# Six weight units split in the opening, whole fp32 products for g, k, r, v of the recurrent mixer, and 512 columns in the last attention's value product

## Chip, core and metric

The kernel runs on one core of one Trainium2 chip. The metric is the device time of one execution in microseconds (us). All data is fp32; 256 tokens, 1024 features.

## The reference, cut to what matters

```
for i in range(2):                                   # first block
    sh1, sc1, gt1, sh2, sc2, gt2 = split(silu(c) @ ada_w[i] + ada_b[i], 6)
    h = rmsnorm(x, norm_g[i, 0]) * (1 + sc1) + sh1
    if i == 0:
        b, c_, hv = split(h @ conv_w_in, 3)
        y = (b * causal_conv3(c_ * hv)) @ conv_w_out
    else:                                            # recurrent mixer
        xr, xw, xk, xv, xa, xg = h + (shift(h) - h) * mu
        r, k, v = xr @ w_r, xk @ w_k, xv @ w_v
        g = sigmoid(xg @ g1) @ g2
        w, a = ...                                   # decay and gate from xw, xa
        y = (group_norm(wkv7_scan(r, w, k, v, ...)) + bonus) * g @ w_o
    x = x + gt1 * y
    h = rmsnorm(x, norm_g[i, 1]) * (1 + sc2) + sh2
    x = x + gt2 * (square(relu(h @ mlp_w1[i])) @ mlp_w2[i])
x = rmsnorm(x, final_g)
x = x + sparse_attention(rms_norm(x)); x = x + sq_relu_mlp(rms_norm(x))
k, v, f = split(rms_norm(x, g_kv) @ w_kv)            # last attention
x = x + softmax_attention(rms_norm(x, g_attn_b) @ w_q, k, v, decay(f)) @ w_o
x = rms_norm(x + sq_relu_mlp(rms_norm(x)))
```

## The kernel before

Features lie on partitions, tokens along the free axis. A weight matrix is cut into units of 128 x 1024: eight tiles of 128 x 128, one for each 128 features that are summed over (kt). Units come from HBM in pairs of 1 MB (`_dma`, L326) into the pool `raw` with two buffers. The code asks for a pair ahead of its use (`DMA_AHEAD`, 2), and all these loads stand in one queue on SP.

Nearly every product is made in three parts. `_split` (L334) rounds a unit to fp32r on ACT (L354, the high half) and subtracts it from the unit on DVE (L356, the low half), both into one buffer `HL` of the pool `hl` (four buffers). The activations are split in the same way. `mm3` (L384) then issues three fp32r products for each tile: high x high, high x low, low x high (L387 to L389). The pool buffer is given back when PE has read it, the raw buffer when DVE has split its second unit. In `rows_gen` (L412) the roles are turned: 128 tokens of the activations are the stationary operand and 256 columns of the weights stream (L423), which gives values by token.

A fp32 product that is not split is one instruction in the code and two records in the profile.

The modulation vectors (`ada`) are matrix by vector products with silu(c). Most run on DVE: one reduction of a 128 x 1024 tile gives one column (`ada_one`, L545, written as a sum in what follows; the profile shows it with a read of the accumulator behind it). Eight of them, the scale tiles of the first layer, run on PE (`ada_pe`, L558): eight tiles of 128 x 128 against a column of silu(c).

The opening, `conv_start` (L581): eight steps, one for each kt. A step sums a scale tile on PE and a shift tile on DVE, makes a column of gain on DVE (L617), normalizes x (L619), makes z on ACT (L621), its high half on ACT (L622) and its low half on DVE (L623). The first six weight units are loaded into tiles of their own (`hs`) and multiplied whole, as fp32, with the whole z (`zf`, L630), as far as the step allows. Then the ordinary loop of the conv goes on with unit 6.

The recurrent mixer, `rwkv` (L1133): the front normalizes x and makes h and its difference to the token before, xx. `mixed` (L1193) makes one kt of an input: xx * mu + h on DVE (L1194), its high half on ACT (L1195), its low half on DVE for g and on POOL for k, r and v (L1196). The units come in the order g (2), k (8), r (8), v (8), then w_o (8). Each k output starts a chain of short steps (`decay`, `front`; the scans are L1253), each r output another (`back`, which begins with L1358), each pair of v outputs starts `values`, which waits for copies and products on POOL (L1452, L1455) and issues L1459, L1467 and L1473 on PE. `inverse` inverts 32 x 32 blocks on DVE, 31 steps of two instructions (L1423, L1425), with transposes at its start (L1418) and end (L1428, L1430). When the inverse and all values are there, eight `state` chains run, four at a time (L1493 is their first product). Between the unit pairs of the mixer, pairs of `ada` tiles for the second layer are loaded into `raw` as well; DVE reduces them where the scheduler finds room.

The last attention, `fox` (L1042): its values are made by `rows_gen` in four groups of 256 columns, from two units each.

The code issues generators side by side; the order on each engine is then set by a list scheduler with priorities. Instructions of an engine run in that order.

## Time and profile before

| | |
|---|---|
| median of 3 runs | 1436.61 us (1433.08 to 1442.31) |
| profiled execution | 1441.53 us |
| its span in the profile | 1439.8 us |
| PE, DVE, ACT, POOL busy | 94%, 71%, 54%, 12% of the span |
| HBM read | 257.69 MB, 180 GB/s over the span |

The profile is of one execution. PE is TensorE, DVE is VectorE, ACT is ScalarE, POOL is GpSimd; SP issues the loads. Times within it are from the start of the span. "L356" is line 356 of the kernel before. Busy shares are means over all stages.

### The profile page before, as it was taken

The numbers are of one execution on the slowest core, as the hardware profiler recorded it, in microseconds if no ns is written. First come the engines' busy times: TensorE is split into PE (matmuls) and PEld (weight loads), VectorE is DVE, ScalarE is ACT, GpSimd is POOL, SyncE is SP. The second block draws the span as 40 slices with busy tenths as digits, with TensorE's granted clock in tenths as the row PEclk, the third lists the DMA queues.
The fourth block names the chain that finished last, engine by engine and source line by source line (L and its number), as shares of the span: only waits on it lengthen the run. The fifth ranks groups of instructions, "written<-read, shape, count | busy, mean of one in ns | idle before, by whom it ended". The sixth has DMA issues, their size and how long they took to land.

```text
span 1439.8 us, 26749 instructions
## 1 busy us (share of the span) xinstructions
PE 1357.8 (94%) x10724; PEld 1303.4 (91%) x10724; DVE 1019.3 (71%) x1959; ACT 772.5 (54%) x1480; POOL 172.8 (12%) x181
## 2 busy tenths in 40 slices
PE   7999999998879869999999998999999999999997
PEld 6899899997779868989999986899999997899997
DVE  3499998756999886678566679765556759565554
ACT  2345664843756431248367555665474557573663
POOL 0000000003783422010000073000000000000000
PEclk9899999998999988999999999999999999999999
DMA  9488888552235552156555543255555651365552
GB/s 371 159 333 286 308 309 303 192 189 104 74 118 197 192 168 74 59 176 212 176 181 197 179 142 117 97 196 185 179 196 182 214 193 64 122 217 188 179 195 97
DMA packets 46908, 263.43 MB, mean 183 GB/s; under 512 B 5472, under 2 KB 9776, under 8 KB 20800
## 3 DMA queue, kind: packets, MB, share of 16 engines
q1 hardware_dynamic: 46432, 260.97, 51.8%
q8 instruction: 84, 1.38, 0.4%
q0 software_dynamic: 208, 0.59, 0.1%
q14 instruction: 40, 0.33, 0.1%
q10 hardware_dynamic: 144, 0.16, 0.0%
HBM read 257.69 MB, written 2.11 MB: 180 GB/s over the span
## 4 chain that ended last, share of the span: by engine, by line
PE 72%; DVE 15%; DMA 4%; POOL 4%; ACT 2%; issue 2%; POOLq 0%; DVEq 0%; SPq 0%; ACTq 0%
PE mm L388 18%; PE mm L387 18%; PE mm L389 18%; DVE HL L356 4%; DMA raw<-in_w_dram 3%; DVE adu L545 2%; PE mm L630 1%; PE ax L558 1%; PE mm L423 1%; PE ax L423 1%; PE ax L847 1%; ACT HL L354 1%; PE ax L630 1%; PE ax L840 1%; POOL R L1455 1%
## 5 line engine op out<-in xcount | busy, mean ns | idle before, releaser
L356 DVE TENSOR_TENSOR HL<-raw,HL 128x1024 fp32r<-128x1024 f32 x372 | 458.1, 1238 | 229.5 <-ACT HL L354 229.0
L354 ACT ACTIVATE HL<-raw 128x1024 fp32r<-128x1024 f32 x372 | 389.4, 1056 | 295.6 <-PE mm L389 221.3
L389 PE MATMUL mm<-zh,HL 128*128 128x256 f32 (+1 forms) x1328 | 376.1, 284 | 5.9 <-DVE HL L356 5.8
L387 PE MATMUL mm<-zh,HL 128*128 128x256 f32 (+1 forms) x1328 | 376.8, 284 | 4.4 <-DVE x L701 1.6
L388 PE MATMUL mm<-zl,HL 128*128 128x256 f32 (+1 forms) x1328 | 375.1, 283 | 0.0
L388 PE MATMUL mm<-hlo,HL 128*128 128x256 f32 x1024 | 287.9, 281 | 0.1
L389 PE MATMUL mm<-hh,HL 128*128 128x256 f32 x1024 | 287.6, 281 | 0.0
L387 PE MATMUL mm<-hh,HL 128*128 128x256 f32 x1024 | 285.3, 279 | 0.0
L387 PEld LDWEIGHTS mm<-zh,HL 128*128 128x128 f32 x1328 | 251.3, 189 | 8.4 <-issue 3.8
L389 PEld LDWEIGHTS mm<-zh,HL 128*128 128x128 f32 x1328 | 251.5, 190 | 7.6 <-DVE HL L356 7.6
L388 PEld LDWEIGHTS mm<-zl,HL 128*128 128x128 f32 x1328 | 252.2, 190 | 0.0
L387 PEld LDWEIGHTS mm<-hh,HL 128*128 128x128 f32 x1024 | 193.3, 189 | 0.0
L388 PEld LDWEIGHTS mm<-hlo,HL 128*128 128x128 f32 x1024 | 192.5, 188 | 0.3 <-DVE hlo L746 0.3
L389 PEld LDWEIGHTS mm<-hh,HL 128*128 128x128 f32 x1024 | 192.4, 188 | 0.0
L515 POOL TENSOR_TENSOR r<-r,mhalf 128x2 f32<-128x2 f32 x6 | 6.3, 1046 | 682.4 <-DVE r L510 545.6
L387 PE MATMUL mm<-yh,HL 128*128 128x256 f32 x272 | 80.1, 297 | 8.2 <-ACT yh L1195 3.9
L545 DVE CUSTOM_DVE_ANT_0 adu<-adu,cact,cols 128x1024 f32<-128x1024 f32 x64 | 81.2, 1280 | 2.0 <-DMA adu<-in_ada_dram 2.0
L388 PE MATMUL mm<-yl,HL 128*128 128x256 f32 x272 | 78.9, 292 | 0.0
L389 PE MATMUL mm<-yh,HL 128*128 128x256 f32 x272 | 78.1, 288 | 0.0
L387 PEld LDWEIGHTS mm<-yh,HL 128*128 128x128 f32 x272 | 52.5, 194 | 10.4 <-ACT yh L1195 4.5
L746 DVE TENSOR_TENSOR hlo<-ma,hh 128x256 fp32r<-128x256 f32 x128 | 53.5, 421 | 5.8 <-ACT hh L743 3.1
L743 ACT ACTIVATE hh<-ma 128x256 fp32r<-128x256 f32 x128 | 52.9, 417 | 3.5
(437 smaller groups left out, 2246.5 us busy)
## 6 DMA issues: line engine op xcount, KB each, us to landing
raw<-in_w_dram SPq DMA_DIRECT2D x187, 1024.0 KB, 5.0
adu<-in_ada_dram SPq DMA_DIRECT2D x72, 512.0 KB, 8.1
raw<-in_ada_dram SPq DMA_DIRECT2D x12, 1024.0 KB, 5.0
hs<-in_w_dram SPq DMA_DIRECT2D x3, 1024.0 KB, 12.6
cb<-cd SPq DMA_DIRECT2D x1, 2048.0 KB, 9.0
rs<-raw SPq DMA_DIRECT2D x28, 64.0 KB, 2.2
x<-in_x_dram SPq DMA_DIRECT2D x4, 256.0 KB, 4.6
R<-in_wa_dram SPq DMA_DIRECT2D x2, 512.0 KB, 6.5
```

What stands on the lines that cost most here:

```text
L354: s.nc.scalar.activation(h, raw, AF.Copy)
L356: s.nc.vector.tensor_tensor(l, raw, h.bitcast(F32), op=OP.subtract)
L387: mm(ps, H[:, kt], rh, start=start, stop=False)
L388: mm(ps, H[:, kt], rl, start=False, stop=False)
L389: mm(ps, L[:, kt], rh, start=False, stop=stop)
L423: s.nc.tensor.matmul(ps[j][:, :256], a, b[:, k], start=kt == i == 0, stop=kt == 7 and i == 2)
L545: s.nc.vector.tensor_tensor_reduce(t, t, s.cact, scale=1.0, scalar=s.c("adab", i), op0=OP.mult, op1=OP.add, accum_out=s.modf[:, i:i + 1])
L558: s.nc.tensor.matmul(ps, w[:, k], s.ccol[:, k:k + 1], start=k == 0, stop=k == KT - 1)
L630: mm(tiles[i][:, :T], w[:, k], zf[:, k], start=k == 0, stop=k == KT - 1)
L743: nc.scalar.activation(s.hh[:, m], a, AF.Copy)
L746: nc.vector.tensor_tensor(s.hlo[:, m], a, s.hh[:, m].bitcast(F32), op=OP.subtract)
L840: tr(pt[:, 128 * j:128 * j + 128], lg[e][:, 128 * j:128 * j + 128], s.ident)
```

## The change

Three edits. In the opening, the six first units are now split like all others (four into the tiles `hs`, two into `HL`), and go through `mm3` with the split z; the products follow z by two steps (`PLAG`). Three of the eight scale tiles (steps 3, 5, 7) are summed on DVE and not on PE. In the recurrent mixer, the 26 units of g, k, r and v are not split: a pair is loaded straight into a buffer of the pool `hl` (named `rawh`), up to three pairs ahead, and multiplied whole, as fp32, with unsplit inputs xg, xk, xr, xv; the copies on ACT and the subtractions on DVE and POOL that split these inputs are gone. In the last attention, the value product runs in two groups of 512 columns.

```diff
-ADAPE = range(8)
+ADAPE = (0, 1, 2, 4, 6)
+PLAG = 2
...
-def row_units(w):
+def row_units(w, n=256):
-    u = w.reshape(2, 4, 128, -1, 256).transpose(3, 0, 2, 1, 4)
+    u = w.reshape(n // 128, D // n, 128, -1, n).transpose(3, 0, 2, 1, 4)
...
-        s.R[p] = s.rawx.pop(p) if p in s.rawx else s.raw.tile([128, 2, D], F32, name="raw")
         n, i = s.pairs[p]
+        if n == "w" and 2 * p in s.whole:
+            s.R[p] = s.hl.tile([128, 2, D], F32, name="rawh", tag="HL")
+        else:
+            s.R[p] = s.raw.tile([128, 2, D], F32, name="raw")
...
-        while s.dma_to <= min(p + s.DMA_AHEAD - 1, len(s.pairs) - 1):
+        while s.dma_to <= min(p + (3 if u in s.whole else s.DMA_AHEAD) - 1, len(s.pairs) - 1):
             s._dma()
         s.split_to += 1
         if s.pairs[p][0] == "ada":
             return
-        if u < s.whole:
+        if u in s.whole:
...
+        if L is None:
+            mm(ps, H[:, kt], rh, start=start, stop=stop)
+            return
...
-    def rows_gen(s, n, z, evac):
+    def rows_gen(s, n, z, evac, N=256):
         for m in range(n):
             ps = [s.mmbank() if RB[(2 * m + j) % len(RB)] else s.axbank() for j in range(2)]
-            for q in range(2):
-                H, L = (w.rearrange("p (k a) m -> p k (a m)", a=2) for w in s.unit())
-                for k in range(4):
-                    kt = 4 * q + k
+            for q in range(N // 128):
+                H, L = (w if w is None else w.rearrange("p (k a) m -> p k (a m)", a=N // 128) for w in s.unit())
+                for k in range(D // N):
+                    kt = D // N * q + k
                     for j in range(2):
-                        zh, zl = (y[:, kt, 128 * j:128 * j + 128] for y in z)
-                        for i, (a, b) in enumerate(((zh, H), (zh, L), (zl, H))):
-                            s.nc.tensor.matmul(ps[j][:, :256], a, b[:, k], start=kt == i == 0, stop=kt == 7 and i == 2)
+                        zs = [y[:, kt, 128 * j:128 * j + 128] for y in z]
+                        ab = [(zs[0], H)] if L is None else [(zs[0], H), (zs[0], L), (zs[1], H)]
+                        for i, (a, b) in enumerate(ab):
+                            s.nc.tensor.matmul(ps[j][:, :N], a, b[:, k], start=kt == i == 0,
+                                               stop=kt == 7 and i == len(ab) - 1)
...
-        hs = [s.big.tile([128, 2, 2, D], F32, name=f"hs{i}", tag=f"h{i}") for i in range(2)]
-        s.rawx = {p: hs[p // 2][:, p % 2] for p in range((GN + 1) // 2)}
-        s.whole = GN
+        hs = [s.big.tile([128, 2, 2, KT, 128], F32R, name=f"hs{i}", tag=f"h{i}") for i in range(2)]
+        s.hlx.update({u: hs[u // 2][:, u % 2] for u in range(4)})
...
-        for kt in range(KT):
-            pm = s.axbank()
-            s.ada_pe(st[kt][0], pm[:, :1])
-            s.ada_one(st[kt][1], 8 + kt)
-            loads(kt + CSP + 1)
-            g = s.gp[:, 0, kt:kt + 1]
-            V.scalar_tensor_tensor(g, pm[:, :1], a1[:, kt:kt + 1], s.c("ng", kt), op0=OP.add, op1=OP.mult)
-            t = s.t("z0")
-            V.tensor_tensor(t, s.x[:, kt], s.rstd[:, :T], op=OP.mult)
-            z = zf[:, kt]
-            A.activation(z, t, AF.Identity, bias=s.mod[:, 0, 1, kt:kt + 1], scale=g)
-            A.activation(s.zh[:, kt, :T], z, AF.Copy)
-            V.tensor_tensor(s.zl[:, kt, :T], z, s.zh[:, kt, :T].bitcast(F32), op=OP.subtract)
-            while len(units) < GN and kt >= CSW[len(units) // 2]:
-                units.append(s.unit(0)[0])
-                at.append(0)
+        for kt in range(KT + PLAG):
+            if kt < KT:
+                g = s.gp[:, 0, kt:kt + 1]
+                if kt in ADAPE:
+                    pm = s.axbank()
+                    s.ada_pe(st[kt][0], pm[:, :1])
+                    V.scalar_tensor_tensor(g, pm[:, :1], a1[:, kt:kt + 1], s.c("ng", kt), op0=OP.add, op1=OP.mult)
+                else:
+                    s.ada_dve(st[kt][0], kt)
+                    V.scalar_tensor_tensor(g, s.modf[:, kt:kt + 1], 1.0, s.c("ng", kt), op0=OP.add, op1=OP.mult)
+                s.ada_one(st[kt][1], 8 + kt)
+                loads(kt + CSP + 1)
+                t = s.t("z0")
+                V.tensor_tensor(t, s.x[:, kt], s.rstd[:, :T], op=OP.mult)
+                z = zf[:, kt]
+                A.activation(z, t, AF.Identity, bias=s.mod[:, 0, 1, kt:kt + 1], scale=g)
+                A.activation(s.zh[:, kt, :T], z, AF.Copy)
+                V.tensor_tensor(s.zl[:, kt, :T], z, s.zh[:, kt, :T].bitcast(F32), op=OP.subtract)
+                while len(units) < GN and kt >= CSW[len(units) // 2]:
+                    units.append(s.unit(0))
+                    at.append(0)
             for i, w in enumerate(units):
-                while at[i] <= kt:
+                while at[i] <= kt - PLAG:
                     k = at[i]
-                    mm(tiles[i][:, :T], w[:, k], zf[:, k], start=k == 0, stop=k == KT - 1)
+                    s.mm3(tiles[i][:, :T], w, k, s.zh[:, k, :T], s.zl[:, k, :T], k == 0, k == KT - 1)
...
-            s.drive(s.rows_gen(4, (zh, zl), ev_vv), per=PERF)
+            s.drive(s.rows_gen(2, (zh, zl), ev_vv, 512), per=PERF)
...
-            gh, gl = s.yh, s.yl
-            new = lambda n, tags, w=T: [s.big.tile([128, KT, w], F32R, name=n + q, tag=q) for q in tags]
-            xkh, xkl = new("xk", ("zh", "zl"), T + 2)
-
-            def mixed(n, kt, hi, lo_, on=None):
-                t = s.t("mx")
-                V.scalar_tensor_tensor(t, xx[:, kt], s.c("mu", 8 * n + kt), h[:, kt, 1:], op0=OP.mult, op1=OP.add)
-                A.activation(hi[:, kt, :T], t, AF.Copy)
-                (on or eng("ml")).tensor_tensor(lo_[:, kt, :T], t, hi[:, kt, :T].bitcast(F32), op=OP.subtract)
-
-            def mixes(n, hi, lo_):
+            new = lambda n, tag: s.big.tile([128, KT, T], F32, name=n, tag=tag)
+            xg, xk, xr = new("xg", "yh"), new("xk", "zh"), new("xr", "yl")
+
+            def mixed(n, kt, out):
+                V.scalar_tensor_tensor(out[:, kt], xx[:, kt], s.c("mu", 8 * n + kt), h[:, kt, 1:], op0=OP.mult, op1=OP.add)
+
+            def mixes(n, out):
                 for kt in range(KT):
-                    mixed(n, kt, hi, lo_)
+                    mixed(n, kt, out)
...
-            s.drive(s.linear_gen(2, lambda k: gh[:, k], lambda k: gl[:, k], ev_g, head=2),
-                    mixes(2, xkh, xkl), per=1)
-            xrh, xrl = new("xr", ("yh", "yl"))
-            side = s.spawn(mixes(0, xrh, xrl))
-            s.linear(8, lambda k: xkh[:, k, :T], lambda k: xkl[:, k, :T], ev_k, head=2, per=PERK)
+            none = lambda k: None
+            s.drive(s.linear_gen(2, lambda k: xg[:, k], none, ev_g, head=2), mixes(2, xk), per=1)
+            side = s.spawn(mixes(0, xr))
+            s.linear(8, lambda k: xk[:, k], none, ev_k, head=2, per=PERK)
...
-            s.linear(8, lambda k: xrh[:, k], lambda k: xrl[:, k], ev_r, head=2, per=PERR)
+            s.linear(8, lambda k: xr[:, k], none, ev_r, head=2, per=PERR)
...
-            s.drive(s.rows_gen(4, (xv[:, 0], xv[:, 1]), ev_v), per=PERV, alone=True)
+            s.drive(s.rows_gen(4, (xv,), ev_v), per=PERV, alone=True)
...
+            us = [u for u in range(s.start["rwkv"], 2 * len(s.pairs)) if s.pairs[u // 2][0] == "w"]
+            s.whole |= set(us[:26])
```

The scheduler then orders the program anew. Three places, all on DVE. First the opening, from the second step's sum on; `z`, `zf`, `zh` and `zl` are as above, `adu` is a modulation tile, `gp` the gain. Before:

```order
L545 ISA adu,mod<-adu,cact,cols 128x1024
L545 ISA mod 128x1
L623 TENSOR_TENSOR zl<-zf,zh 128x256
L545 ISA adu,mod<-adu,cact,cols 128x1024
L545 ISA mod 128x1
L617 SCALAR_TENSOR_TENSOR gp<-ax,a_136,cols 128x1 x2
L623 TENSOR_TENSOR zl<-zf,zh 128x256
L545 ISA adu,mod<-adu,cact,cols 128x1024
L545 ISA mod 128x1
L623 TENSOR_TENSOR zl<-zf,zh 128x256
L545 ISA adu,mod<-adu,cact,cols 128x1024
L545 ISA mod 128x1
```

The same place of the changed kernel (its L553 is L545 of before, L638 is L623, L627 is L617, L359 is L356, L630 is the gain column of a tile summed on DVE):

```order
L553 ISA adu,mod<-adu,cact,cols 128x1024
L553 ISA mod 128x1
L638 TENSOR_TENSOR zl<-zf,zh 128x256
L359 TENSOR_TENSOR hs_114<-raw,hs_114 128x1024
L627 SCALAR_TENSOR_TENSOR gp<-ax,a_138,cols 128x1
L359 TENSOR_TENSOR hs_114<-raw,hs_114 128x1024
L553 ISA adu,mod<-adu,cact,cols 128x1024
L553 ISA mod 128x1
L553 ISA adu,mod<-adu,cact,cols 128x1024
L553 ISA mod 128x1
L638 TENSOR_TENSOR zl<-zf,zh 128x256
L630 SCALAR_TENSOR_TENSOR gp<-mod,cols 128x1
```

The two splits of the first pair stand around a gain column, and the sum of step 3 behind the one of step 2.

Second, the start of the k part of the mixer; `gA` is the scan's output, `mx` an input of k or r, `gs` the gate g, `th` and `Sd` belong to the decay. Before:

```order
L1253 SCALAR_TENSOR_TENSOR gA<-one_3618,th 128x64 x4
L1255 TENSOR_TENSOR Sd<-gA 128x260
L1194 SCALAR_TENSOR_TENSOR mx<-hx,cols 128x256
L1259 TENSOR_TENSOR PC<-Sd,gA 128x3
L1194 SCALAR_TENSOR_TENSOR mx<-hx,cols 128x256
L356 TENSOR_TENSOR HL<-raw,HL 128x1024
L1194 SCALAR_TENSOR_TENSOR mx<-hx,cols 128x256 x4
L1317 TENSOR_SCALAR gs<-gt 128x256 x2
L1194 SCALAR_TENSOR_TENSOR mx<-hx,cols 128x256 x4
L356 TENSOR_TENSOR HL<-raw,HL 128x1024
L1253 SCALAR_TENSOR_TENSOR gA<-one_3618,th 128x64 x4
```

The same place now (L1263 is L1253 of before, L1265 is L1255, L1327 is L1317, `raw` is a modulation tile):

```order
L1263 SCALAR_TENSOR_TENSOR gA<-one_3700,th 128x64 x4
L553 ISA raw,mod<-raw,cact,cols 128x1024
L553 ISA mod 128x1
L1265 TENSOR_TENSOR Sd<-gA 128x260
L553 ISA raw,mod<-raw,cact,cols 128x1024
L553 ISA mod 128x1
L1269 TENSOR_TENSOR PC<-Sd,gA 128x3
L1327 TENSOR_SCALAR gs<-gt 128x256
L553 ISA raw,mod<-raw,cact,cols 128x1024
L553 ISA mod 128x1
L1327 TENSOR_SCALAR gs<-gt 128x256
L553 ISA raw,mod<-raw,cact,cols 128x1024
```

The mixes have moved ahead of the scan (all eight of r stand there), the splits are gone, and modulation sums stand in their place.

Third, the end of the inverse; `it` and `ya` are its steps, `hk` its result. Before:

```order
L545 ISA raw,mod<-raw,cact,cols 128x1024
L545 ISA mod 128x1
L1423 TENSOR_TENSOR it<-ya 128x60
L545 ISA raw,mod<-raw,cact,cols 128x1024
L545 ISA mod 128x1
L1425 TENSOR_TENSOR ya<-ya,it 128x2x30
L1423 TENSOR_TENSOR it<-ya 128x31
L1425 TENSOR_TENSOR ya<-ya,it 128x31
L1428 STREAM_TRANSPOSE hk<-ya 128x32x32
L1430 STREAM_TRANSPOSE hk<-ya 128x32x32
```

The same place now (L1432 is L1423 of before, L1434 is L1425, L1461 is L1452, L1437 and L1439 the transposes):

```order
L1434 TENSOR_TENSOR ya<-ya,it 128x3x29
L1432 TENSOR_TENSOR it<-ya 128x60
L1434 TENSOR_TENSOR ya<-ya,it 128x2x30
L1432 TENSOR_TENSOR it<-ya 128x31
L1461 COPY yb<-R 64x4x64
L1434 TENSOR_TENSOR ya<-ya,it 128x31
L1437 STREAM_TRANSPOSE hk<-ya 128x32x32
L1461 COPY yb<-R 64x4x64
L1439 STREAM_TRANSPOSE hk<-ya 128x32x32
```

The sums are gone from between the steps; two copies for the last values stand there.

## Rows read from the trace of the kernel before

**Rows 1.** Busy time by stage: start:end, length, each engine's busy us (instructions), clock, DMA.

```profile
14.00:64.00 50.00, 47.15 (x224) 40.63 (x224) 19.66 (x43) 12.00 (x22) 0.00 (x0) 0.86 0.60 245
64.00:150.00 86.00, 80.51 (x657) 78.43 (x656) 80.10 (x146) 42.53 (x72) 0.00 (x0) 1.00 0.88 317
150.00:336.00 186.00, 181.68 (x1517) 180.61 (x1517) 144.87 (x222) 107.15 (x172) 3.87 (x6) 1.00 0.70 247
336.00:358.00 22.00, 17.09 (x81) 14.66 (x82) 15.40 (x36) 9.79 (x23) 8.71 (x17) 0.77 0.26 103
358.00:421.00 63.00, 49.81 (x347) 43.22 (x346) 59.84 (x127) 40.25 (x99) 52.13 (x57) 0.95 0.23 79
421.00:470.00 49.00, 48.40 (x419) 48.08 (x420) 46.30 (x87) 34.89 (x93) 20.98 (x23) 1.00 0.55 201
470.00:527.00 57.00, 40.98 (x303) 40.12 (x304) 49.84 (x103) 22.96 (x61) 23.80 (x15) 0.87 0.58 191
...
925.00:1120.00 195.00, 194.74 (x1646) 194.52 (x1645) 121.26 (x169) 115.75 (x196) 0.00 (x0) 1.00 0.56 190
```

**Rows 2.** The chain that ended last, opening: start us, us, what.

```profile
48.47 5.61 PE ax L630 x26
```

**Rows 3.** Groups by line: busy us, mean ns of one, idle before.

```profile
L356 DVE TENSOR_TENSOR HL<-raw,HL 128x1024 fp32r<-128x1024 f32 x372 | 458.1, 1238 | 229.5 <-ACT HL L354 229.0
L354 ACT ACTIVATE HL<-raw 128x1024 fp32r<-128x1024 f32 x372 | 389.4, 1056 | 295.6 <-PE mm L389 221.3 <-DMA raw<-in_w_dram 65.3 <-PE ax L423 8.1
...
L545 DVE CUSTOM_DVE_ANT_0 adu<-adu,cact,cols 128x1024 f32<-128x1024 f32 x64 | 81.2, 1280 | 2.0 <-DMA adu<-in_ada_dram 2.0
```

**Rows 4.** Timeline of the opening: start us, us, engine, line, what [idle before].

```profile
13.99 6.83 PE L558 MATMUL ax<-ccol,adu 128*128 128x1 f32 x32
...
19.63 0.33 SPq L331 DMA_DIRECT2D hs<-in_w_dram  x1
...
24.39 0.43 DVE L623 TENSOR_TENSOR zl<-zf,zh 128x256 fp32r<-128x256 f32 x1 [1.12 <-ACT zh L622]
...
26.68 4.01 PE L558 MATMUL ax<-ccol,adu 128*128 128x1 f32 x32
...
28.94 0.22 DVE L617 SCALAR_TENSOR_TENSOR gp<-ax,a,cols 128x1 f32<-128x1 f32 x1 [2.92 <-PE ax L558]
...
61.07 2.36 DVE L356 TENSOR_TENSOR HL<-raw,HL 128x1024 fp32r<-128x1024 f32 x2 [0.52 <-ACT HL L354]
```

**Rows 5.** DMA issues of the page: issues, KB each, median us to landing.

```profile
raw<-in_w_dram SPq DMA_DIRECT2D x187, 1024.0 KB, 5.0
```

**Rows 6.** k part alone, by line: splits L356, mixes L1194, sums L545, subtractions L1196.

```profile
358.00:421.00 63.00, 14.05 (x10) 0.95 0.23 79
...
358.00:421.00 63.00, 7.77 (x13) 0.95 0.23 79
...
358.00:421.00 63.00, 3.52 (x4) 0.95 0.23 79
...
358.00:421.00 63.00, 0.00 (x0) 13.12 (x15) 0.95 0.23 79
```

**Rows 7.** Waits in the value part, 470 to 527: us in total, times, longest.

```profile
PE ax L1493 <- DVE hk L1430: 8.8, 1, 8.8
...
PE ax L1459 <- POOL R L1455: 7.2, 3, 2.7
```

**Rows 8.** The chain that ended last, end of the value part: start us, us, what.

```profile
506.04 0.71 POOL yb L1452
...
506.87 0.79 POOL yb L1452
...
507.72 3.32 POOL R L1455
...
526.72 3.75 PE ax L1493 x16
...
533.36 0.89 PE ax L1500 x8
```

More of the change, by code (lines that the diff above doesn't have):

```diff
@@ L38 @@
 VW = 0
-ML5 = [0, 0, 0, 0, 0, 0, 0, 0]
 ADE = [0, 0]
@@ L42 @@
 RB = [1, 0]
-ENG = {'db': 1, 'zb': 1, 'ta': 0, 'kr': 1, 'ts': 1, 's1': 0, 'yl': 0, 'sd': 0, 'kp': 1, 'rk': 0, 'zk': 0, 'ab': 1, 's0': 1, 'ml': 1}
+ENG = {'db': 1, 'zb': 1, 'ta': 0, 'kr': 1, 'ts': 1, 's1': 0, 'yl': 0, 'sd': 0, 'kp': 1, 'rk': 0, 'zk': 0, 'ab': 1, 's0': 1}
 GN = 6
-ADAPE = range(8)
+ADAPE = (0, 1, 2, 4, 6)
 CSP = 4
 CSW = [1, 3, 5]
+PLAG = 2
 HLB = 4
@@ L166, in fox_units @@
     w = I["w_kv_b_2"]
-    return (units_of(w[:, :D]) + row_units(w[:, D:2 * D]) + units_of(I["w_q_b_2"][0]) + units_of(I["w_o_b_2"][0]))
+    return (units_of(w[:, :D]) + row_units(w[:, D:2 * D], 512) + units_of(I["w_q_b_2"][0]) + units_of(I["w_o_b_2"][0]))
 def att_consts():
@@ L347, in _split @@
             pool = s.hle if u < s.early and u % 3 == 2 and HLE else s.hl
-            t = pool.tile([128, 2, KT, 128], F32R, name="HL")
+            t = pool.tile([128, 2, KT, 128], F32R, name="HL", tag="HL")
         s.H[u], s.L[u] = t[:, 0], t[:, 1]
@@ L542, in ada_load, with ada_dve, ada_one @@
         return t
-    def ada_one(s, t, i):
+    def ada_dve(s, t, i):
         s.nc.vector.tensor_tensor_reduce(t, t, s.cact, scale=1.0, scalar=s.c("adab", i), op0=OP.mult, op1=OP.add,
                                          accum_out=s.modf[:, i:i + 1])
+    def ada_one(s, t, i):
+        s.ada_dve(t, i)
         q, part = i % 8, i // 8 % 6
@@ L1096, in ev_vv @@
                 for j in range(2):
-                    A.activation(vr[:, 2 * m:2 * m + 2, j], ps[j][:, :T].rearrange("p (a n) -> p a n", a=2), AF.Copy,
+                    A.activation(vr[:, 4 * m:4 * m + 4, j], ps[j].rearrange("p (a n) -> p a n", a=4), AF.Copy,
                                  scale=s.rcol[:, j:j + 1])
-            s.drive(s.rows_gen(4, (zh, zl), ev_vv), per=PERF)
+            s.drive(s.rows_gen(2, (zh, zl), ev_vv, 512), per=PERF)
             s.new_y()
@@ L1186, in rwkv @@
             s.norm_close()
-            s.new_y()
-            gh, gl = s.yh, s.yl
-            new = lambda n, tags, w=T: [s.big.tile([128, KT, w], F32R, name=n + q, tag=q) for q in tags]
-            xkh, xkl = new("xk", ("zh", "zl"), T + 2)
-            def mixed(n, kt, hi, lo_, on=None):
-                t = s.t("mx")
-                V.scalar_tensor_tensor(t, xx[:, kt], s.c("mu", 8 * n + kt), h[:, kt, 1:], op0=OP.mult, op1=OP.add)
-                A.activation(hi[:, kt, :T], t, AF.Copy)
-                (on or eng("ml")).tensor_tensor(lo_[:, kt, :T], t, hi[:, kt, :T].bitcast(F32), op=OP.subtract)
-            def mixes(n, hi, lo_):
+            new = lambda n, tag: s.big.tile([128, KT, T], F32, name=n, tag=tag)
[3 more added lines that the diff above has]
+            def mixes(n, out):
                 for kt in range(KT):
-                    mixed(n, kt, hi, lo_)
+                    mixed(n, kt, out)
                     yield None
@@ L1218, in rwkv @@
                 mm(pl[:, :T], wam[:, kt], xx[:, kt], start=False, stop=kt == KT - 1)
-                mixed(5, kt, gh, gl, (V, G)[ML5[kt]])
+                mixed(5, kt, xg)
             A.activation(lo[0:64], pl[0:64, :T], AF.Tanh)
@@ L1344, in mix_v @@
                     s.finish_gen(fro[p])
-                xv.append(s.big.tile([128, 2, KT, T], F32R, name="xv", tag="h1"))
+                xv.append(new("xv", "h1"))
                 for kt in range(KT):
-                    mixed(3, kt, xv[0][:, 0], xv[0][:, 1])
+                    mixed(3, kt, xv[0])
                     yield WV
@@ L1635, in run @@
         s.feed = lambda kt: None
-        s.hlx, s.rawx, s.whole = {}, {}, 0
+        s.hlx, s.whole = {}, set()
+        if "rwkv" in s.start:
+            us = [u for u in range(s.start["rwkv"], 2 * len(s.pairs)) if s.pairs[u // 2][0] == "w"]
+            s.whole |= set(us[:26])
         s.early = next((s.start[n] for n in stages if n not in ("conv", "mlp0")), 2 * len(s.pairs))
```

## Prediction

> **What bounds the kernel now.** I read the page first, then the busy time by stage, then the groups, and last the timeline, the waits and the chain of the stages that the change touches. On the page PE is busy nearly throughout, but that is a mean over stages that differ [rows 1]. In the plain matmul stages, such as 925 to 1120, PE does nothing but stream: 1646 records in 194.74 us, 0.118 us for one product of 256 columns. In 14 to 64, the opening, PE is busy 47.15 of 50 us and DVE 19.66: PE sets the pace. In 64 to 150, the conv, DVE is busy 80.10 of 86: DVE sets the pace, so whatever the opening gains or loses is handed on. From 150 to 336 PE is full again and DVE has 41 us free. The recurrent mixer has four parts: its front (336 to 358, a chain of short steps), the k part (358 to 421, DVE 59.84 of 63), the r part (421 to 470, PE 48.40 of 49, DVE nearly as full) and the value part (470 to 527, DVE 49.84 of 57, PE full for a part only). After 527 eight states run, a chain of short PE and DVE steps.
>
> **Price of one product.** A whole fp32 product of 256 columns is two records. Twenty-six of them back to back took 5.61 us, 0.216 us each [rows 2], so a product costs 0.43 us against 3 x 0.118 = 0.35 for the three split ones. A unit of eight costs PE 0.63 us more whole, and spares DVE 1.24 and ACT 1.06 us of splitting [rows 3].
>
> **The opening, term 1: -5 us.** PE loses three of eight modulation sums (two tiles took 4.01 us [rows 4], so 6 us in all) and 6 x 0.63 = 4 us of products, and is no longer the bound. DVE gets three sums at 1.28 and six splits at 1.24, 11 us, and becomes it. I follow its new order with the durations of the rows. ACT can split unit 0 only behind z of step 1 (that step's subtraction starts at 24.39 [rows 4]), so its high half is there at 25.5; the third tile's sum stands behind the first product of it on PE, and at the pace of PE's first two sums (6.83 us for two) it ends at 28.9. That is where the third gain column came before, 28.94, so to there nothing is won. Then DVE splits unit 1 (to 30.4), which frees the raw buffer. Of two raw buffers, the third pair of units therefore goes out at 30.4, not at 19.63 [rows 4]; it lands some 5 us later [rows 5] and the four modulation tiles queued behind it on SP by about 40.5. DVE wants the first of them near 49, so this is hidden by 8 us. From 30.4 DVE has nine sums (11.5 us), six splits (7.4), six subtractions of 0.43 (2.6) and five columns of 0.22 (1.1), 22.6 us up to the split of unit 7. Three of the subtractions wait 1.12 us for ACT, as the one at 24.39 does; the others stand behind a second sum. Three pairs of splits wait another 0.6. That is 22.6 + 5.2, and ends at 58.2. Before, the same split ended at 61.07 + 2.36 = 63.43. I take -5. The ends are -10 (no wait at all) and 0 (PE at its slow level throughout, so that each column comes late).
>
> **The mixer's front, term 2: +2 us.** 24 mixes instead of 11 now stand ahead of the first scan: 13 x 0.6 = 7.8 us at the k part's mean [rows 6], less eight subtractions of 0.43, and one modulation sum stands ahead of the norm's factor. DVE was busy 15.40 of 22 us [rows 1], so most of these 4 to 6 us goes into its gaps. Bounds 0 and +5.5.
>
> **The k part, term 3: -2 us.** DVE loses ten splits, 14.05 us [rows 6], and eleven mixes at 0.6, 6.6 us. But where four records of modulation sums stood there (two sums, 3.52 us), the new order has fifteen. At 1.28 us each, as where POOL is quiet, the thirteen add 16.6 us; at the 1.76 of this part they add 22.9. So DVE changes by -4 to +2. POOL loses fifteen subtractions, 13.12 of its 52.13 us, which leaves DVE alone more often. I take -2. PE's work grows by some 92 whole products for 276 split ones, 92 x 0.076 = 7 us, in a part where it is busy 49.81 of 63; DVE hides it.
>
> The sums took 1.76 us each beside a busy POOL here [rows 6] and 1.28 in the mean of all in the span [rows 3]. The Trainium skill, SBUF, section "Who interferes with whom", says that a DVE instruction with two SBUF inputs is held off for the whole of a GpSimd instruction that reads SBUF and has started first. That speaks against moving sums into this part. The trace agrees in kind: 0.48 us more, about half of a mean POOL instruction (52.13 us for 57, 0.91 each). The full hold is the first rival.
>
> **The r part, term 4: +6 us.** PE is the bound, and between the first product of an r back end and the first of a value step the order has 180 split products before and 64 whole ones now: 27.5 - 21.2 = +6.3. DVE loses seven splits and three of six sums by its order, but it was not alone at the limit and can give PE little. Bounds 0 (DVE was as tight as PE) and +8.
>
> **The value part, term 5: -11.5 us.** Before, it ran from 469.1 to 526.72. PE's last wait in it is 8.8 us for the inverse on DVE [rows 7]. Fourteen modulation sums and five splits stood between the inverse's steps, and now three splits do: DVE has 14 x 1.28 + 2 x 1.24 = 20.4 us less to do, and the inverse ends near the last values. The value steps before that took 48.8 us in four rounds; in each PE waited for POOL, 7.2 us in three waits [rows 7], since two copies (0.71 and 0.79 us) and two products (3.32 us) on POOL stand between two rounds, about 5 us with their hand-overs [rows 8], and PE had only 36 products (4.2 us) to put there. Now it has twelve whole ones, 5.2 us: most of the 44 x 0.43 - 132 x 0.118 = +3.3 us goes into these waits. Rounds of 12.5, 12.5, 12 and 7 us give 44, and about 2 more until the state starts. So 46 instead of 57.6. Ends: -5.5 (the rounds stay as long and get the 3.3 us) and -15 (no waits left).
>
> **The states, term 6: -2.5 us.** After the long wait PE ran at 1.2 GHz: sixteen records took 3.75 us, against 0.89 for eight at 2.4 GHz a little later [rows 8]. With that wait gone some 24 records win 0.12 us each. Three splits and two sums on DVE go too, in a chain that waits for DVE only in part. Bounds -5 and +1.
>
> **The last attention's values, term 7: -1 us.** 192 products of 256 columns cost 192 x 0.118 = 22.7 us, and 96 of 512 columns cost between 96 x 0.216 (a record that streams as many columns) and 96 x 0.236: -1.9 to 0. The Trainium skill, TensorE: Matmul & The Clock Gate, section "Back-to-back issue gap", puts N columns at N / 2.4 + 2.5 ns, an estimate of 0.216 us; by it the term would be -1.9 and the total one us lower. No row shows a product of 512 columns.
>
> Sum: -5 + 2 - 2 + 6 - 11.5 - 2.5 - 1 = -14. The profiled execution took 1441.5 us (span 1439.8 and 1.7 around it), 4.9 above the median of the runs; it would take 1427.5, and the median 1436.6 - 14 = 1422.6.
>
> **Rivals.** (a) POOL holds each of the thirteen sums for a whole instruction: 13 x (1.28 + 0.91) = 28.5 us less 20.6 that go, and the k part grows by 8 instead of falling by 2: -4, 1432.6. For it: DVE is in order and the scans behind the sums feed ACT and PE. Against: rows 6 show 1.76. Chance 0.1. (b) PE stays the bound in the value part too: term 5 is -5.5 and the states win nothing: -5.5, 1431. For it: PE was busy 89 of the 106 us of both parts [rows 1] and now gets 9.6 us more in a shorter time. Chance 0.14. (c) More is won: the k part's chain of short steps was slowed by POOL as a whole and gives 8 us, and the opening 8: -23, 1413.6. Chance 0.2. (d) Slower: SP is one queue. Whole tiles wait there for a buffer that PE frees, the next pair of sums is loaded behind them, and the sums stand in DVE's order ahead of scans. If DVE reaches a pair before PE has freed the tile, DVE and all behind it wait out a load of 5 us; six pairs give +30, and the total is +16, 1452.6. It decides as soon as PE frees a pair of k tiles less often than DVE takes two sums, every 8.4 us (63 us for fifteen). Against: PE was busy 49.81 us of the 63 [rows 1] and gets 7 more, so it still has room. Chance 0.08.
>
> **How the numbers follow.** The forecast (-14, its own range -7 to -21, 1415.6 to 1429.6) has 0.48. The range 1409 to 1437 takes in (a), (b) and most of (c), leaves (d) out and about one case in ten at the lower end. About 1%, 14.4 us, can be told from no change: 1422.2 is that bound. Of the forecast 0.27 lies below it and 0.21 above; (c) is faster; (a) and (b) are within; (d) is slower. Faster 0.47, same 0.45, slower 0.08.
>
> **What would show it.** The first split product of the ordinary conv loop near 58 to 60 us, right behind the split that ended at 63.43 before (term 1). First scan of the mixer to first r back end 60 to 63 us long, with sums at 1.3 to 1.7 us (term 3). From there to the first value step about 54 us (term 4), and the state's first product 46 us after that with a wait under 2 us ahead of it (term 5). Wrong would be: DVE waiting for a DMA of modulation tiles in the k part, a wait for the inverse that stays, or a conv stage that no longer follows the opening.

## The result, and the profile after

The changed kernel took 1426.85 us (median of 7 runs, 1418.36 to 1428.91) against 1439.44 us for the kernel before beside it: ratio 0.991 (95% interval 0.9886 to 0.9933), 12.6 us less. A second series of it (9 runs, below) gave 1426.69 us and 0.9922 (0.9896 to 0.9947). 1422.6 was forecast. The total fell close to the forecast; its terms did not, as the stages show.

The changed kernel, busy time by stage, columns as in [rows 1]; the stretches begin and end where the same instructions do as there, the last but one is the eight `state` chains, called the states from here on:

```profile
14.00:64.00 50.00, 42.79 (x250) 41.52 (x249) 33.05 (x59) 18.75 (x30) 0.00 (x0) 1.00 0.69 259
64.00:150.00 86.00, 80.66 (x651) 79.15 (x652) 80.67 (x149) 43.26 (x72) 1.68 (x1) 0.98 0.87 315
331.20:353.20 22.00, 15.81 (x64) 12.92 (x65) 18.67 (x45) 5.71 (x13) 8.49 (x16) 0.77 0.45 177
353.20:417.70 64.50, 53.38 (x255) 42.77 (x253) 53.05 (x132) 26.96 (x75) 40.73 (x49) 0.94 0.63 228
417.70:474.40 56.70, 56.14 (x361) 52.90 (x362) 34.77 (x82) 23.48 (x74) 6.09 (x7) 0.95 0.27 93
474.40:514.70 40.30, 39.56 (x266) 36.53 (x264) 34.10 (x67) 21.53 (x61) 11.22 (x15) 1.00 0.17 57
514.70:558.60 43.90, 41.47 (x323) 38.17 (x324) 30.25 (x75) 8.13 (x22) 9.94 (x8) 1.00 0.15 46
905.00:1100.00 195.00, 194.86 (x1646) 194.64 (x1646) 121.35 (x170) 115.86 (x197) 0.00 (x0) 1.00 0.55 189
```

Four readings. In the opening DVE is busy 33.05 us instead of 19.66 and PE 42.79 instead of 47.15, at a granted clock of 1.00 instead of 0.86. In the k part neither PE (53.38 of 64.5) nor DVE (53.05, it was 59.84 of 63) is full any more, and yet it is not shorter. In the r part PE is full, 56.14 of 56.7. In the value part PE is full too, 39.56 of 40.3, where it had 40.98 of 57. The plain matmul stage of the last row is as it was.

The profiled execution is the fastest of the seven (1418.36 us, span 1416.6). The profile of the second series (1429.77 us, span 1428.0) is of the slowest of its nine, 3.1 us above their median, so the sizes of the parts are read from both. "k part" is from the first scan to the first r back end, "r part" from the first product of that back end to the first value step, "value part" from there to the state's first product, "states" to the end of the last product of that line (L1493, now L1502). The half microsecond between the k part's end on DVE and the r part's start on PE is in neither.

| us | before | after, 1st | after, 2nd | 2nd - before | forecast |
|---|---|---|---|---|---|
| start to first scan | 358.0 | 353.2 | 356.9 | -1.1 | -3 (terms 1, 2) |
| k part | 62.6 | 64.5 | 64.8 | +2.2 | -2 |
| r part | 48.0 | 56.1 | 58.4 | +10.4 | +6 |
| value part | 57.6 | 40.3 | 40.3 | -17.3 | -11.5 |
| states | 52.2 | 43.9 | 49.8 | -2.4 | -2.5 |
| behind the states | 860.9 | 858.0 | 857.3 | -3.6 | -1 |
| span | 1439.8 | 1416.6 | 1428.0 | -11.8 | -14 |

The value part in the profile after, PE's first products of each round (start us, us, engine, line, what, idle before):

```profile
474.39 1.95 PE L1468 MATMUL ax<-R,yb 128*128 128x128 f32 x16
...
486.21 1.95 PE L1468 MATMUL ax<-R,hk 128*128 128x128 f32 x16
...
498.03 1.95 PE L1468 MATMUL ax<-R,yb 128*128 128x128 f32 x16
...
508.66 0.46 PE L1468 MATMUL ax<-R,hk 128*128 128x128 f32 x2 [0.37 <-ACT hk L1453]
...
514.67 1.16 PE L1502 MATMUL ax<-hk,ed 128*128 128x128 f32 x8 [0.27 <-DVE R L1477]
```

Rounds of 11.8, 11.8, 10.6 and 6.0 us: this is PE's own work, with no wait for POOL. Where PE stood 8.8 us for the inverse [rows 7], 0.27 us are left.

### The profile page after: what moved, and what is told of

It reads as the page before. It is cut to its first block, busy times and chain, and to the rows that moved or that the text cites. A ratio compares the mean times of both kernels' runs of the same rounds, so it can differ in the third digit from the quotient of the medians.

```text
span 1416.6 us, 26025 instructions
## 1 busy us (share of the span) xinstructions
PE 1349.4 (95%) x10420; PEld 1290.1 (91%) x10420; DVE 994.1 (70%) x1937; ACT 742.4 (52%) x1424; POOL 132.9 (9%) x157
## 4 chain that ended last, share of the span: by engine, by line
PE 76%; DVE 13%; POOL 3%; DMA 3%; issue 2%; ACT 2%; POOLq 0%; DVEq 0%; SPq 0%; ACTq 0%
PE mm L394 19%; PE mm L393 19%; PE mm L395 19%; DVE HL L359 3%; PE mm L391 2%; DVE adu L553 2%; PE mm L430 2%; PE ax L430 1%; DMA raw<-in_w_dram 1%; DMA adu<-in_ada_dram 1%; PE ax L569 1%; PE ax L862 1%; POOL R L1321 1%; PE ax L1372 1%; DMA rs<-raw 1%
## 5 line engine op out<-in xcount | busy, mean ns | idle before, releaser
L359 DVE TENSOR_TENSOR HL<-raw,HL 128x1024 fp32r<-128x1024 f32 x348 | 426.8, 1233 | 226.0 <-ACT HL L357 225.7
L357 ACT ACTIVATE HL<-raw 128x1024 fp32r<-128x1024 f32 x348 | 364.3, 1056 | 281.5 <-PE mm L395 214.9
L553 DVE CUSTOM_DVE_ANT_0 adu<-adu,cact,cols 128x1024 f32<-128x1024 f32 x67 | 84.9, 1280 | 0.6 <-DMA adu<-in_ada_dram 0.6
L393 PE MATMUL mm<-yh,HL 128*128 128x256 f32 x256 | 75.5, 297 | 3.1 <-DVE x L718 2.2
L394 PE MATMUL mm<-yl,HL 128*128 128x256 f32 x256 | 74.2, 292 | 0.0
L395 PE MATMUL mm<-yh,HL 128*128 128x256 f32 x256 | 73.8, 289 | 0.0
```

The costliest lines, as they stand in the source:

```text
L357: s.nc.scalar.activation(h, raw, AF.Copy)
L359: s.nc.vector.tensor_tensor(l, raw, h.bitcast(F32), op=OP.subtract)
L393: mm(ps, H[:, kt], rh, start=start, stop=False)
L394: mm(ps, H[:, kt], rl, start=False, stop=False)
L395: mm(ps, L[:, kt], rh, start=False, stop=stop)
L553: s.nc.vector.tensor_tensor_reduce(t, t, s.cact, scale=1.0, scalar=s.c("adab", i), op0=OP.mult, op1=OP.add, accum_out=s.modf[:, i:i + 1])
```

## The experiments

Each kernel was timed in five rounds beside the kernel before; a difference to before in us is the ratio less one, times the median of before in that series. A difference between two changed kernels is that of their medians.

### The three edits one by one

open_alone is the kernel before with this and what belongs to it in the opening:

```diff
-ADAPE = range(8)
+ADAPE = (0, 1, 2, 4, 6)
+PLAG = 2
...
+        s.hlx.update({u: hs[u // 2][:, u % 2] for u in range(4)})
...
+                    s.mm3(tiles[i][:, :T], w, k, s.zh[:, k, :T], s.zl[:, k, :T], k == 0, k == KT - 1)
```

> The kernel before with the opening edit alone (six split tiles, five sums on PE, lag of two). Theory A, the parts are separate: the shift of 4 us that the two traces show from 60 us on is made here and carried to the end, so -4 us against before (-3 to -5.5). Rival B: the front of the mixer waits for something of its own, so that the shift is lost at 340 us: -1 to +1 us. The first split product of the conv loop behind a split that ends near 60.6 us in both.

1433.96 us against 1440.29: 0.9965 (0.9944 to 0.9985), -5.0 us. Theory A. Its first scan stands at 354.3 us, 3.7 early.

mixer_alone is the kernel before with the mixer's edit:

```diff
+            s.whole |= set(us[:26])
...
-            s.linear(8, lambda k: xkh[:, k, :T], lambda k: xkl[:, k, :T], ev_k, head=2, per=PERK)
+            s.linear(8, lambda k: xk[:, k], none, ev_k, head=2, per=PERK)
```

> The kernel before with whole g, k, r, v products in the mixer alone. Theory A, the parts add up: of -12.6 us in the medians 4 are the opening's and 1 to 2 the last attention's, so -7 us here (-5 to -10), made of about +2 in the k part, +5 to +8 in the r part and -17 in the value part. Rival B, the opening is worth nothing by the end: -11 to -13 us here.

1426.96 us: 0.9914 (0.9886 to 0.9943), -12.4 us: B's size, though B's reason, an opening that is worth nothing, is against open_alone. Its k, r and value part took 64.6, 56.1 and 40.3 us, as in the whole change: these are the mixer's own. Its first scan stands at 358.2 us, against 358.0 before, so the longer front of the mixer costs nothing that shows.

fox_alone is the kernel before with this:

```diff
-    return (units_of(w[:, :D]) + row_units(w[:, D:2 * D]) + ...
+    return (units_of(w[:, :D]) + row_units(w[:, D:2 * D], 512) + ...
...
-            s.drive(s.rows_gen(4, (zh, zl), ev_vv), per=PERF)
+            s.drive(s.rows_gen(2, (zh, zl), ev_vv, 512), per=PERF)
```

> The kernel before with 512 columns in the last attention's value product alone. The products themselves: 96 x 0.230 against 192 x 0.118 us is -0.5 us. Theory A: only that, -0.5 us (0 to -1). Rival B: the 2.4 us by which the two traces differ near 1240 us come from this edit too (PE's two waits at the start of the last MLP, 1.3 and 0.7 us, go): -2.4 us (-1.8 to -3).

1440.29 us: 0.9999 (0.998 to 1.0017), nearer to theory A; the interval, -2.9 to +2.4 us, does not exclude B. The two waits near 1240 us, 1.3 and 0.7 us before, are down to 0.4 in its trace, but they are 0.2 in mixer_alone and gone in sums_early, which do not have this edit.

The parts give -17.4 us, the whole -11 to -13: the intervals allow both sums. xv_no_open, below, asks again.

### What shortened the value part

Two things changed there at once: the products are whole, and the modulation sums are gone. Each was tried without the other. sums_late is the changed kernel with the pairs of sums in the buffers of the whole tiles, in stream order:

```diff
-        if n == "w" and 2 * p in s.whole:
+        if n == "ada" or 2 * p in s.whole:
```

> The changed kernel with the pairs of modulation tiles in the buffers of the whole tiles, so that they queue in the order of the stream and 17 of the sums stand between the steps of the inverse again. Theory A, the value part shrank because these sums left DVE there: 17 x 1.28 = 22 us come back to a DVE that is busy 34 of 40 us, the value part goes from 40 to about 54 us, the k part gains at most 2, and the kernel is 10 us slower than the changed one (8 to 14), within 3 us of before. Rival B, it shrank because whole products fill PE's waits for POOL and five splits are gone, whatever DVE does between: within 2 us of the changed kernel.

1437.26 us: 0.9978 (0.9958 to 0.9997), 10.4 us above the changed kernel. The value part and the states of sums_late, by stage:

```profile
471.60:525.70 54.10, 40.31 (x266) 36.57 (x264) 50.64 (x96) 22.30 (x62) 17.03 (x15) 0.94 0.58 202
525.70:579.90 54.20, 52.28 (x323) 46.45 (x324) 32.30 (x79) 7.69 (x20) 9.94 (x8) 0.78 0.09 30
```

DVE is busy 50.64 of 54.10 us again, as it was before, and PE's waits in the value part show the inverse (L1439) again, but little of POOL, which before took 7.2 us of them:

```profile
PE ax L1502 <- DVE hk L1439: 8.5, 1, 8.5
...
PE ax L1468 <- POOL R L1464: 1.5, 1, 1.5
```

Theory A, with the value part and the total where it had them (about 54 us, and 10 slower).

sums_early is the kernel before, split products and all, with the twelve pairs ahead of the units of k and r:

```diff
-ADAPOS = [0, 0, 0, 0, 0, 1, 0, 1, 1, 1, 0, 0, 7, 1, 0, 0, 0]
+ADAPOS = [0, 0, 2, 2, 2, 2, 2, 2, 0, 0, 0, 0, 0, 0, 0, 0, 0]
```

> The kernel before, with split products as before, but the twelve pairs of modulation tiles placed ahead of the units of k and r, so that no sum stands between the steps of the inverse. Theory A, what shortened the value part is that the sums left it: value part 57.6 to about 46 us (42 to 49), the wait for the inverse gone and the slow-clock stretch in the states with it (states 44 to 46 instead of 52), while k and r part grow by 8 to 18 together, since DVE is as good as full there with the splits in it; in all -4 us against before (-10 to +3). Rival B, whole products are what shortens it: value part 54 us or more.

1442.63 us against 1439.08: 1.0035 (1.001 to 1.0061), +5.0 us. Theory A in the mechanism, but only there: the value part is shorter still than its 42 to 49 us, the k and r part grow by more than its 8 to 18, the states do not fall to 44 to 46, and the total lies outside its range. sums_early by stage, k part to states:

```profile
359.30:433.00 73.70, 57.12 (x317) 48.35 (x316) 68.03 (x139) 39.16 (x97) 62.37 (x62) 0.72 0.35 122
433.00:490.20 57.20, 51.39 (x441) 50.45 (x440) 53.49 (x100) 36.67 (x92) 18.92 (x18) 1.00 0.61 212
490.20:528.90 38.70, 37.01 (x310) 35.94 (x308) 37.41 (x79) 25.38 (x66) 11.24 (x15) 1.00 0.38 119
528.90:582.50 53.60, 50.84 (x323) 44.92 (x324) 31.13 (x76) 7.68 (x20) 9.94 (x8) 0.81 0.11 34
```

In its value part PE waits 1.1 us for DVE and 0.4 us for ACT, and for POOL not at all.

The four kernels side by side, from one profile each; the two with whole products have the new opening as well, which ends ahead of these parts:

| us | k part | r part | value part | sum |
|---|---|---|---|---|
| split, sums late (before) | 62.6 | 48.0 | 57.6 | 168.2 |
| split, sums early | 73.7 | 56.6 | 38.7 | 169.0 |
| whole, sums late | 62.8 | 58.3 | 54.1 | 175.2 |
| whole, sums early (the change) | 64.5 | 56.1 | 40.3 | 160.9 |

The value part depends on where the sums stand (-18.9 and -13.8) and hardly on the products (+1.6 and -3.5). But with splits in it DVE has no room for the sums earlier: it is busy 68.03 of 73.70 us in the k part, and k and r part grow by 19.7, which eats the gain. Whole products free that room (moving the sums costs k and r part nothing: 121.1 with them late, 120.6 early) and lengthen these two parts by 10 us instead. In the changed kernel more than half of that goes with a wait and is not the price of the products, as xv_free shows below. In these three parts neither half alone gains anything; only both do.

### Why the k part did not get shorter

The waits of PE and DVE in the k part of the changed kernel (engine, line, waited for: us, times, longest):

```profile
PE ax L1295 <- ACT ksq L1286: 4.9, 2, 4.7
PE ax L1314 <- ACT ne L1310: 2.8, 1, 2.8
...
DVE xv L1206 <- POOL R L1321: 5.2, 1, 5.2
```

And its end in the timeline:

```profile
415.35 1.51 POOL L1321 TENSOR_TENSOR R<-txt 64x256 f32<-64x256 f32 x2
...
416.90 0.88 DVE L1206 SCALAR_TENSOR_TENSOR xv<-hx,cols 128x256 f32<-128x256 f32 x2 [5.16 <-POOL R L1321]
417.70 0.42 DVE L1367 TENSOR_TENSOR R<-mm,R 128x256 f32<-128x256 f32 x1
...
418.26 0.98 PE L1372 MATMUL ax<-R 128*128 128x128 f32 x3 [3.94 <-DVE R L1367]
```

DVE's next instruction mixes v's input into the tile that POOL still reads for the last of the k chains (`txt`, L1321). DVE's instructions run in their order, so the first r back end (L1367) stands behind it, and PE behind that. The expectation below calls these ends of the k chains back ends too. xv_free takes another tile:

```diff
-                xv.append(new("xv", "h1"))
+                xv.append(new("xv", "yh"))
...
-            ya = s.big.tile([128, 2, 1024], F32, name="ya", tag="yh")
+            ya = s.big.tile([128, 2, 1024], F32, name="ya", tag="h1")
```

> The changed kernel with the mixed input of v in the tile that the input of g has left, not in the one that the k part's back ends still read (the inverse takes that one instead). Theory A, the k part ends late because DVE, in order, waits 5.2 us for POOL ahead of the first r back end: the first r back end comes 3 to 5 us earlier (k part 60 to 61.5), the r part is as long as it was, and the kernel is 4 us faster than the changed one (2 to 6). Rival B, PE has its r products to do anyway and the end of the r part does not move: k part shorter, r part longer by as much, 0 us (-1 to +1).

1418.76 us: 0.9862 (0.9836 to 0.9888), 7.9 us below the changed kernel in the same series: theory A, and more than its 2 to 6. The k part is 60.1 us. From the first r back end to the first value step, and the states, by stage:

```profile
413.50:468.80 55.30, 55.30 (x370) 51.77 (x370) 31.16 (x73) 23.39 (x74) 9.65 (x13) 1.00 0.33 124
...
508.70:559.80 51.10, 49.18 (x325) 43.37 (x324) 29.18 (x73) 8.44 (x22) 11.69 (x10) 0.83 0.13 39
```

From its first product, at 415.5 us, the r part is 53.3 us at the full clock, against 56.1 and 58.4 behind the wait; from the first r back end on DVE it is 55.3, against 56.7 and 58.9. From the first scan to the first value step xv_free takes 115.4 us and the changed kernel 121.2 and 123.7, so 6 to 8 us are won between these two points. In the four profiles with the wait and whole products (both of the changed kernel, mixer_alone, sums_late) PE stands 3.9 to 4.6 us there and the r part has a mean granted clock of 0.91 to 0.95; in xv_free and xv_no_open, without it, 1.00. So the wait costs a stretch at the slow clock as well.

xv_no_open is xv_free with the opening of before:

```diff
-ADAPE = (0, 1, 2, 4, 6)
-PLAG = 2
+ADAPE = range(8)
```

> The kernel with the free tile for v's mixed input, but with the opening of before (six whole units, eight sums on PE). It asks again what the opening is worth beside a changed mixer. Theory A, the parts add: 4 to 5 us slower than the same kernel with the new opening (1418.8 us), so 1422 to 1425 us, with the first scan near 358 us instead of 353. Rival B, the time that the opening wins is lost again in slow-clock stretches of the conv and the first MLP: within 2 us of it.

1424.01 us, 0.9896 (0.9871 to 0.9921): 5.3 us above xv_free, and a first scan at 359.4 us instead of 353.4: theory A. The opening is worth about 5 us alone and beside this mixer.

### The r part

r_split_early is the changed kernel with r in split products, and the sums placed as in sums_early:

```diff
+            xrh, xrl = (s.big.tile([128, KT, T], F32R, name="xr" + q, tag=q) for q in ("yh", "yl"))
...
-            s.linear(8, lambda k: xr[:, k], none, ev_r, head=2, per=PERR)
+            s.linear(8, lambda k: xrh[:, k], lambda k: xrl[:, k], ev_r, head=2, per=PERR)
...
-            s.whole |= set(us[:26])
+            s.whole |= set(us[:10] + us[18:26])
```

> The changed kernel with r in split products again (eight units, eight subtractions on POOL) and the pairs of sums placed ahead of k and r, so that none falls into the value part. Theory A, the r part's +8 us is the price of 64 whole products on a PE that is the bound: 64 x 0.078 = 5 us come back over k and r part, some 4 of them in the r part (56.1 to 52), the k part pays 0 to 2 for splits and subtractions: -3 us against the changed kernel (-6 to 0). Rival B, the r part is as long because of its chain of small products and waits: r part 55 to 57 us, and the kernel 0 to 3 us slower for the work on DVE and POOL.

1419.97 us: 0.9876 (0.9848 to 0.9904), 6.7 us below the changed kernel, but by neither theory. The k part got shorter (60.6 us), the r part did not (58.3). The run changes the products and the place of the sums at once, and does not say what each is worth. DVE in the r part of r_split_early:

```profile
412.95 0.41 DVE L1377 TENSOR_TENSOR R<-mm,R 128x256 f32<-128x256 f32 x1
419.53 1.28 DVE L1207 SCALAR_TENSOR_TENSOR xv<-hx,cols 128x256 f32<-128x256 f32 x3 [6.17 <-POOL R L1330]
420.72 0.42 DVE L1393 TENSOR_TENSOR tm<-ax,rc 128x256 f32<-128x256 f32 x1
```

The wait for POOL has only moved: two r back ends now stand ahead of it, and their masks (L1393) behind. r_split_low gives these mixes a lower priority:

```diff
-                    mixed(3, kt, xv[0])
+                    with s.prio(-150):
+                        mixed(3, kt, xv[0])
```

> The kernel with r in split products and early sums, and with the mixes of v at a lower priority, so that one sum and the first masks of the first back end stand ahead of the first mix on DVE, which waited 6.2 us for POOL there and held up the back ends. Theory A, this wait was why the r part stayed at 58.3 us for all its cheaper products: 2 to 3.5 us of it go, the r part is 55 to 56 us, and the kernel 2.5 us faster (1 to 4), near 1417.5 us. Rival B, PE has enough to do beside the wait: r part 58 us, the same time within 1 us.

1414.66 us: 0.9827 (0.9803 to 0.985), 5.3 us less and the lowest median of all: theory A, and more than its 1 to 4. The r part is 54.2 us (55 to 56 forecast), though DVE still waits 5.12 us: the first masks now stand ahead of the wait, PE has their products meanwhile, and its own longest wait in the part falls from 3.1 to 2.0 us. It is no shorter than in xv_free with whole products (53.3), so what split products alone are worth in r stays open.

```profile
416.38 0.43 DVE L1408 SCALAR_TENSOR_TENSOR ed<-tm,rc 128x128 f32<-128x128 f32 x1
421.93 0.48 DVE L1207 SCALAR_TENSOR_TENSOR xv<-hx,cols 128x256 f32<-128x256 f32 x1 [5.12 <-POOL R L1330]
```

### The changed kernel again

after_again is the changed kernel, unaltered.

> The changed kernel once more, unaltered. The parts alone gave -5.0 (opening), -12.4 (mixer) and 0.0 us (last attention), -17.4 in all, where the change as a whole had -12.6 in 7 runs. Theory A, the parts add up and the first series fell high: -15 to -18 us against before. Rival B, the opening's 4 to 5 us are not worth their size in the whole: -12 to -13.5. In either case k part 64.5, r part 56.1, value part 40.3 and states 43.9 us as in the first profile, and the difference to that profile's short end lies in slow-clock stretches behind 600 us.

1426.69 us against 1439.08: 0.9922 (0.9896 to 0.9947), -11.2 us, a smaller gain than in either range, and nearer to B. Its profile is the column "after, 2nd" of the table above; r part, value part and states by stage:

```profile
422.20:480.60 58.40, 58.37 (x361) 54.59 (x362) 34.33 (x80) 23.46 (x74) 6.10 (x7) 0.91 0.26 91
480.60:520.90 40.30, 39.56 (x266) 36.51 (x264) 34.11 (x67) 21.54 (x61) 11.23 (x15) 1.00 0.19 57
520.90:570.70 49.80, 47.59 (x323) 42.47 (x324) 30.56 (x75) 8.24 (x22) 9.95 (x8) 0.86 0.13 41
```

Of the 11.4 us between the two profiles of this kernel 5.9 lie in the states, 2.3 in the r part and 3.7 ahead of the mixer; the instructions are the same. Behind 600 us, where the difference was expected, there is none (857.3 and 858.0 us behind the states). In the states and the r part the granted clock differs (1.00 and 0.86; 0.95 and 0.91).

## Why the prediction was right, and where it was not

The total was right within its own range, and in part by luck: against the second profile the k and the r part came out 8.6 us too long and the start 1.9, the value part 5.8 too short and what lies behind the states 2.6. Numbers are of the first profile unless said.

**Opening and front, terms 1 and 2 (-5 and +2): nearly right, one wait missed.** The split of unit 7 was to end at 58.2 us and ended at 60.7 (half of the four in the last row of the first block below), against 63.43 before. The conv's first product (second block, the changed kernel, then before) came 3.7 us early. What was missing to 58.2 are DVE's waits for gain columns behind PE's sums: I counted only the waits for ACT and gave the third tile's sum its place, but not the fifth's, 3.50 us, nor the seventh's, 0.98.

```profile
29.39 0.22 DVE L627 SCALAR_TENSOR_TENSOR gp<-ax,a,cols 128x1 f32<-128x1 f32 x1 [2.84 <-PE ax L569]
...
42.68 0.22 DVE L627 SCALAR_TENSOR_TENSOR gp<-ax,a,cols 128x1 f32<-128x1 f32 x1 [3.50 <-PE ax L569]
...
58.29 4.64 DVE L359 TENSOR_TENSOR HL<-raw,HL 128x1024 fp32r<-128x1024 f32 x4 [0.52 <-ACT HL L357]
```

```profile
60.50 0.28 PE L393 MATMUL mm<-zh,HL 128*128 128x256 f32 x1
...
64.17 0.47 PE L387 MATMUL mm<-zh,HL 128*128 128x256 f32 x1
```

The front cost nothing that shows, where +2 was put: 0.2 us in mixer_alone. The first scan came 4.8 us early in the first profile and 1.1 in the second. Alone and beside xv_free the opening measured 5 us.

**k part, term 3 (-2): wrong, +1.9 to +2.2 in three profiles.** The failed step is to take the part's change from DVE's balance of work alone ("DVE changes by -4 to +2", "I take -2"), as if DVE still set its length. That held for the kernel before; once DVE was relieved (53.05 of 64.5 us), the end of the part was POOL's steps of the last k chains and DVE's wait for them, 5.16 us. I had asked what DVE would lose and gain, not what is late next. Without the wait, in xv_free, k and r part together are 4.3 us longer than before (115.4 against 111.1), and terms 3 and 4 had said +4. The sums themselves cost less than feared. The fifteen sums of this part, with their reads, in the row of that line alone:

```profile
353.20:418.00 64.80, 20.19 (x30) 0.94 0.62 227
```

That is 1.35 us each, where a hold of a mean POOL instruction for each sum would have made it 2.2: rival (a) did not come. But the mean says little of a hold, since eleven of the sums stand ahead of 385 us, where POOL is busy 13.90 of 31.8 us, against 26.84 of 33 behind it: six of the fifteen met no POOL instruction at all and took 1.27 to 1.28 us. Two ran wholly beside two-input products on POOL:

```profile
390.81 1.57 DVE L553 CUSTOM_DVE_ANT_0 raw<-raw,cact,cols 128x1024 f32<-128x1024 f32 x1
...
409.99 1.75 DVE L553 CUSTOM_DVE_ANT_0 raw<-raw,cact,cols 128x1024 f32<-128x1024 f32 x1
...
409.74 2.57 POOL L1321 TENSOR_TENSOR R<-txt 64x256 f32<-64x256 f32 x2
```

They took 0.3 and 0.5 us more. The full hold of the Trainium skill (SBUF, "Who interferes with whom") is not what these rows show: the second sum started 0.25 us behind a pair of POOL products and was done 0.57 us ahead of their end. The pair took 2.57 us, against 1.51 for a pair alone.

**r part, term 4 (+6): right in kind.** PE is full there. At the full clock, in xv_free, the part is 53.3 us, +5.3, or from the first r back end on DVE 55.3 against 48.5, +6.8; +6.3 was worked out. The other 1 to 5 us of the changed kernel come with a granted clock of 0.95 and 0.91 behind PE's wait of 3.94 us. I had not seen that wait, so not its effect on the clock.

**Value part, term 5 (-11.5): the mechanism right, the size too small, -17.3.** Sums out, wait for the inverse gone, the inverse (ends at 509.1) no longer last: shown by sums_late and sums_early. I took 12.5 us for a round and 2 us until the state starts; the rounds were 11.8, 11.8, 10.6 and 6.0 and the wait 0.27. I had left part of POOL's 7.2 us standing; nothing of it was left. But the credit was given in part wrongly: I let whole products fill the waits for POOL. They do (1.5 us are left in sums_late), but the split kernel with early sums has none either, and a value part of 38.7 us.

**States, term 6 (-2.5): the reason wrong, the size luck.** It measured -8.3 in the first profile, outside the bounds, and -2.4 in the second. I took the slow stretch for a consequence of the long wait ahead of it. sums_early has its inverse done before the last values, and its states still take 53.6 us at a mean granted clock of 0.81.

**Last attention, term 7 (-1): about half of it in the trace, nothing that the runs can tell.** The value product of the changed kernel, then of the kernel before (line, form, count: min/median/max ns, first and last start):

```profile
L430 PE MATMUL mm<-HL,zh x32: 388/393/398, 1129.5 to 1150.6; 128*128 128x512 f32 x32
...
L430 PE MATMUL ax<-HL,zl x16: 389/394/396, 1130.7 to 1151.5; 128*128 128x512 f32 x16
```

```profile
L423 PE MATMUL mm<-HL,zh x64: 276/280/288, 1149.7 to 1171.7; 128*128 128x256 f32 x64
...
L423 PE MATMUL ax<-HL,zl x32: 279/281/290, 1150.2 to 1172.2; 128*128 128x256 f32 x32
```

From the first to the last start 22.0 us now and 22.5 before. 22.0 / 95 is 0.232 us a product: the upper bound (0.236) was nearly it, and 0.216 was not reached.

**Rivals.** (b) fell half: PE is the bound of the value part, but at 40 us, not 52. (c) fell: no k part of -8. (d) did not come in the k part; in xv_free DVE does wait 4.4 us for a pair of sums, in an r part in which PE is full, and it costs PE nothing. What remains open is whether the opening is worth its 5 us in the change itself: the parts add to -17.4 and the whole measured -11.2 and -12.6, with intervals of 3 to 4 us on each side.

## What to carry to other kernels

When work is taken off the engine that bounds a stage, follow what is next in that engine's order: an in-order wait for a buffer that another engine still reads, covered before, becomes the end of the stage, and another tile can then be worth much (7.9 us here, where the whole change measured 11 to 13). A price on one engine can be an entry ticket on another: dearer products paid because they made room for other work to leave the stage that could not bear it, and each half alone was worth nothing in the three parts. Not all of them are needed for that: the fastest kernel here has r split again. Read a stage's length together with its granted clock before giving a cause for it.
